# Recurrent stage of a two-block transformer: inverses of 16 x 16 diagonal blocks by substitution on VectorE, moved through DRAM

## The chip, the cores and the metric

The kernel runs on one core of a Trainium2 chip. The metric is the device time of one execution in microseconds. All times below are in microseconds unless marked ns; a time such as 1224.23 is counted from the start of the profiled span.

## The reference

The program is one forward pass of a block with attention and an expert layer, then two further layers. The change touches the mixer of the first of these, which has a recurrent part (8 heads of 64) and a "stick-breaking" attention (8 heads) side by side:

```
def step(state, inp):
    r_t, w_t, k_t, v_t, kk_t, a_t = inp
    sa = jnp.einsum('bhij,bhj->bhi', state, -kk_t)
    state = (state * w_t[:, :, None, :] + sa[..., None] * (kk_t * a_t)[:, :, None, :]
             + v_t[..., None] * k_t[:, :, None, :])
    return state, jnp.einsum('bhij,bhj->bhi', state, r_t)
...
_, y = lax.scan(step, state0, (tm(r), tm(decay), tm(k), tm(v), tm(kk), tm(a)))
```

The sequence has 256 tokens. The kernel does the scan in two chunks of 128 tokens. Within a chunk each head needs the inverse of a unit triangular 128 x 128 matrix I + N, where N holds the products of kk and of kk * a for pairs of tokens, strictly on one side of the diagonal.

## The kernel before

All of this is in `stage_hyb`. Eight heads and two chunks give 16 matrices; they are handled as four groups `(t, g)`, chunk t and head parity g, of four matrices j side by side in a [128, 4, 128] tile.

The stage first runs projections on TensorE: `w_hr` and its small companions, then `w_hq` (queries and keys of the stick attention, `lin_b`, evicted to `sqkT`) and `w_hv` (its values, `lin_a`, into `acc` banks and then `sv`). Their weights come by SP's DMA queue into three `raw` buffers; ScalarE copies each piece of 1024 columns to `hi`, VectorE subtracts to get `lo` (L303), and both must be there before TensorE uses the piece. A further load is issued once the buffer of three loads earlier has been split. While the projections run, VectorE makes the decay-weighted keys and queries `bet`, `kti`, `kap`.

After the projections two streams are written side by side, step by step: `stick()`, with for each of 8 heads the steps logits (tile `psb`), sums (`psc` from `ab`) and values (`sbo`), and `chain()`. `chain()` computes N by `scores` (four groups of four products, masked by `upS` into `NT`), makes the inverses of the diagonal blocks of 2 by a mask, and then doubles the block: for b = 2, 4, 8, 16, 32 there are a product with N (`psq`, L1407, masked into `room`), a product with the transposed inverse (`pst`, L1413, subtracted from `T`), and sixteen transposes that renew `TT` (`ptt`, L1419). A shorter last level joins blocks of 64. Then three more sets of `scores` give the matrices with which rows, states and outputs are computed (`psrh`, `psu`, `pss`, `psy`), interleaved with the output projection `pho`.

A scheduler orders the instructions of each engine over the whole stage by its own estimates; what it chose is shown below as it stands in the built programs. Within one engine, and within SP's queue, instructions run in that order, and one that waits holds all behind it. From `rows_of` on TensorE's order is written by hand.

GpSimd applies two masks to every stick head (`keep`, `nb`; the matrices `ntri`, `nones` are made there too) and computes the output gate (`gadd`, `gv`).

Of the kernel before, what the change touches and what calls it, by code (L numbers as in the profile page):

```python
# [13 lines left out]
F32 = mybir.dt.float32  # L14
# [6 lines left out]
OP = mybir.AluOpType  # L21
# [164 lines left out]
def block_kernel(ctx: ExitStack, tc: tile.TileContext, a: dict, out: bass.AP, start=0, stop=99):  # L186
    nc = tc.nc
# [17 lines left out]
    def bank(name="bank"):  # L205
        return pp.tile([128, 512], F32, name=name, tag="bank")
# [10 lines left out]
    def col(name, j=0, n=None):  # L217
        o, w = COLS[name]
        return cols[:, o + j:o + j + (n or 1)]
# [214 lines left out]
    class Prep:  # L434


        full = None
# [700 lines left out]

    def stage_hyb():
        DEC = math.exp(-0.5)  # L1140
        LEVELS = (2, 4, 8, 16, 32, 64)
        with ExitStack() as es:
            per = es.enter_context(pool("hper", 1))
            esB = ExitStack()
# [16 lines left out]

            upS = tri("upS", OP.is_gt, 1)
            upI = tri("upI", OP.is_ge, 1)

            b2n = per.tile([128, 64, 2], F32, name="b2n")
            G.memset(b2n, 0.0)
            G.affine_select(out=b2n[:, :, 1], in_=b2n[:, :, 1], pattern=[[-2, 64]], compare_op=OP.not_equal, fill=-1.0, base=0, channel_multiplier=1)
            b2n = b2n.rearrange("p a b -> p (a b)")

            lm = {}  # L1170
            for b in LEVELS[:-1]:
# [24 lines left out]
            qkT = per.tile([128, 8, 256], F32, name="sqkT")  # L1196
            sv = per.tile([128, 2, 512], F32, name="sv")
            oT = (per.tile([128, 4, 256], F32R, name="hoTh"), per.tile([128, 4, 256], F32R, name="hoTl"))
            bet = pb.tile([128, 4, 256], F32, name="bet")
            kti = pb.tile([128, 4, 256], F32, name="kti")  # L1200

# [39 lines left out]


            sig = pc.tile([128, 4, 256], F32, name="sig")
            at = bet
            for m in range(4):
                ps = bank("pslw")
                ps_2 = bank("psla")
# [48 lines left out]
            for b in range(2):  # L1296
                ps = bank("psnb")
                for m in range(2):
                    T.matmul(ps[:, m * 256:(m + 1) * 256], sel[:, 2 * b + m, :], rnT, start=True, stop=True)
                V.tensor_tensor(out=kap[:, 2 * b:2 * b + 2, 0, :], in0=kap[:, 2 * b:2 * b + 2, 0, :],  # L1300
                                in1=ps.rearrange("p (m n) -> p m n", m=2), op=OP.mult)

            for m in range(4):
                V.tensor_scalar(out=tmp[:, m, :], in0=at[:, m, :], scalar1=-1.0, scalar2=col("k_a", m), op0=OP.add, op1=OP.mult)
            V.scalar_tensor_tensor(out=kti, in0=tmp, scalar=1.0, in1=kti, op0=OP.add, op1=OP.mult)
            V.tensor_tensor(out=bet, in0=kk, in1=at, op=OP.mult)
            iE = expo(L3, DEC)
            V.tensor_tensor(out=bet, in0=bet, in1=iE, op=OP.mult)
            eX = expo(sig, -DEC)
            V.tensor_tensor(out=kk, in0=kk, in1=eX, op=OP.mult)  # L1310

            for m in range(4):
                V.scalar_tensor_tensor(out=tmp[:, m, :], in0=kap[:, m, 1, :], scalar=col("r_k", m), in1=kti[:, m, :], op0=OP.mult, op1=OP.mult)
# [19 lines left out]
            def cons_qk(m0, mc, ps):  # L1333
                V.tensor_tensor(out=qkT[:, m0:m0 + mc, :], in0=ps.rearrange("p (m n) -> p m n", n=256),
                                in1=rb().unsqueeze(1).to_broadcast([128, mc, 256]), op=OP.mult)

            lin_b("w_hq", 8, 8, 2, xT, cons_qk, bank=acc)

# [8 lines left out]
            ch2 = esD.enter_context(pool("hch2", 2))  # L1347

            table = tc.keep_in_program_order(nc.scalar.preload_act_table_set("natural_log_exp_and_others"))
            TG = [(t, g) for t in range(2) for g in range(2)]  # L1350
            po_ = lambda g: slice(g * 64, (g + 1) * 64)
            b4 = lambda m: m.unsqueeze(1).to_broadcast([128, 4, 128])
            j4 = lambda ps: ps.rearrange("p (j n) -> p j n", j=4)

            room = hT.tile([128, 2, 16, 128], F32, name="room", tag="T8")
            room = [room[:, n] for n in range(2)]
# [1 line left out]
            def mat(name, tag=None):  # L1358
                return ch.tile([128, 4, 128], F32, name=name, tag=tag or name)

            def mat2(i, t, g):

                return room[i][:, 4 * (2 * t + g):4 * (2 * t + g) + 4, :]

            def scores(l, r, t, g):

                ps = bank("psc")
                ts = slice(t * 128, (t + 1) * 128)
                for j in range(4):
                    T.matmul(ps[:, j * 128:(j + 1) * 128], l(j)[po_(g), ts], r(j)[po_(g), ts], start=True, stop=True)  # L1370
                return j4(ps)

            vb, vk = (lambda j: bet[:, j, :]), (lambda j: kti[:, j, :])
            vq, vr = (lambda j: kap[:, j, 0, :]), (lambda j: kap[:, j, 1, :])
            NT, Tm, TT, Bm, LB, LK, U = {}, {}, {}, {}, {}, {}, {}
            btk, htk = ch.tile([128, 512], F32, name="btk"), ch.tile([128, 512], F32, name="htk")

            def chain():

                for t, g in TG:  # L1380
                    ps = scores(vb, vq, t, g)
                    NT[t, g] = mat(f"NT{t}{g}")
                    V.tensor_tensor(out=NT[t, g], in0=ps, in1=b4(upS), op=OP.mult)
                    TT[t, g] = mat(f"TT{t}{g}")
                    V.tensor_tensor(out=TT[t, g], in0=NT[t, g], in1=b4(b2n), op=OP.mult)
                    V.tensor_tensor(out=TT[t, g], in0=TT[t, g], in1=b4(ident), op=OP.add)
                yield
                for t, g in TG:
                    ps = bank("ptt")
                    for j in range(4):  # L1390
                        T.transpose(ps[:, j * 128:(j + 1) * 128], TT[t, g][:, j, :], ident)
                    Tm[t, g] = mat(f"T{t}{g}")
                    A.copy(out=Tm[t, g], in_=j4(ps))
                yield
                to_tok(bet, btk, 0)
                to_tok(kti, htk, 0)
                yield
                for b in LEVELS[:-1]:
                    nb = 64 // b
                    half = lambda x, h: x.rearrange("p j (c h s) -> p j c h s", h=2, s=b)[:, :, :, h, :]  # L1400
                    Q = {}
                    for t, g in TG:
                        Q[t, g] = mat2(0, t, g)
                        G.memset(half(Q[t, g], 1), 0.0)
                        ps = bank("psq")
                        for j in range(4):
                            T.matmul(ps[:, j * 128:(j + 1) * 128], NT[t, g][:, j, :], Tm[t, g][:, j, :], start=True, stop=True)  # L1407
                        V.tensor_tensor(out=half(Q[t, g], 0), in0=half(j4(ps), 0), in1=lm[b].unsqueeze(1).to_broadcast([128, 4, nb, b]), op=OP.mult)
                    yield
                    for t, g in TG:  # L1410
                        ps = bank("pst")
                        for j in range(4):
                            T.matmul(ps[:, j * 128:(j + 1) * 128], TT[t, g][:, j, :], Q[t, g][:, j, :], start=True, stop=True)  # L1413
                        V.tensor_tensor(out=half(Tm[t, g], 0), in0=half(Tm[t, g], 0), in1=half(j4(ps), 0), op=OP.subtract)
                    yield
                    for t, g in TG:
                        ps = bank("ptt")
                        for j in range(4):
                            T.transpose(ps[:, j * 128:(j + 1) * 128], Tm[t, g][:, j, :], ident)  # L1419
                        A.copy(out=TT[t, g], in_=j4(ps))  # L1420
                    yield
                lo, hi = slice(0, 64), slice(64, 128)
                for t, g in TG:
                    Q[t, g] = mat2(0, t, g)
                    ps = bank("psq")
                    for j in range(4):
                        T.matmul(ps[hi, j * 64:(j + 1) * 64], NT[t, g][lo, j, hi], Tm[t, g][lo, j, lo], start=True, stop=True)
                    A.copy(out=Q[t, g][hi, :, 0:64], in_=ps[hi, 0:256].rearrange("p (j n) -> p j n", j=4))
                yield
                for t, g in TG:  # L1430
                    ps = bank("pst")
                    for j in range(4):
                        T.matmul(ps[lo, j * 64:(j + 1) * 64], Q[t, g][hi, j, 0:64], TT[t, g][hi, j, hi], start=True, stop=True)
                    A.activation(out=TT[t, g][lo, :, hi], in_=ps[lo, 0:256].rearrange("p (j n) -> p j n", j=4), func=AF.Copy, scale=-1.0)
                yield
                for dst, l, r, m, tag in ((Bm, vk, vq, upS, None), (LK, vk, vr, upI, "T"), (LB, vb, vr, upI, "NT")):
                    for t, g in TG:
                        ps = scores(l, r, t, g)
                        d = dst[t, g] = mat(f"B{t}{g}", f"{tag}{t}{g}") if tag else mat2(1, t, g)
                        if dst is LB:  # L1440
                            A.copy(out=d, in_=ps)
                            G.affine_select(out=d, in_=d, pattern=[[0, 4], [1, 128]], compare_op=OP.is_ge, fill=0.0, base=0, channel_multiplier=-1)
                        else:
                            V.tensor_tensor(out=d, in0=ps, in1=b4(m), op=OP.mult)
                yield
# [617 lines left out]
```

## Time and profile before

| what | value |
|---|---|
| median of 3 runs (lowest to highest) | 1897.76 (1897.35 to 1899.72) |
| profiled execution, its own time | 1900.1 |
| its span | 1897.9 |
| TensorE busy | 1841.0 (97% of the span) |
| VectorE busy | 1467.2 (77%) |
| ScalarE busy | 998.5 (53%) |
| GpSimd busy | 119.5 (6%) |
| granted TensorE clock, mean | 0.986 of full |

The profiler records one execution. Busy time is the time in which an engine had an instruction under way; TensorE's matmuls overlap, so their durations add up to more than the time that passes, and the time of a step is read from one start to the next. The granted clock is 1.0 at 2.4 GHz and 0.5 at 1.2 GHz.

### The profile page before, as it was taken

How to read it: one execution, taken by the hardware profiler on the slowest of the kernel's cores; microseconds unless marked ns; L12 is line 12 of the kernel's file. 1: busy time of each engine (PE TensorE's matmuls, PEld its weight loads, DVE VectorE, ACT ScalarE, POOL GpSimd, SP SyncE). 2: the span in 40 equal slices, each digit the busy share in tenths (PEclk: the TensorE clock that was granted, in tenths of full speed). 3: DMA queues.
4: the chain of work that ended last, by engine and by line, in shares of the span. 5: the costliest groups of instructions: out<-in, count | busy, mean ns of one | idle time of the engine just before them, and what ended most of it. 6: DMA issues, size and time to landing. Idle time of an engine off the chain costs nothing.

```text
span 1897.9 us, 28745 instructions
## 1 busy us (share of the span) xinstructions
PE 1841.0 (97%) x10944; PEld 1559.8 (82%) x10944; DVE 1467.2 (77%) x3076; ACT 998.5 (53%) x1702; POOL 119.5 (6%) x195
## 2 busy tenths in 40 slices
PE   8999979799999999999999999999999999999997
PEld 6777769798888888888888898898788889688886
DVE  7786766989999887888776588544787888687787
ACT  6566455333555555555555454442555566665555
POOL 0000003330000000000000202222000000000000
PEclk9999999999999999999999999999999999999999
DMA  7442533344555555555555543101455544155552
GB/s 272 168 156 92 177 120 112 112 140 172 178 178 178 178 178 178 178 179 190 179 195 179 190 164 127 68 7 51 150 193 185 173 169 166 71 186 180 197 178 100
DMA packets 43754, 296.13 MB, mean 156 GB/s; under 512 B 4896, under 2 KB 5040, under 8 KB 10208
## 3 DMA queue, kind: packets, MB, share of 16 engines
q1 hardware_dynamic: 41872, 289.35, 43.9%
q0 software_dynamic: 1184, 3.89, 0.7%
q8 instruction: 86, 1.41, 0.3%
q10 hardware_dynamic: 560, 1.05, 0.1%
q14 instruction: 52, 0.43, 0.1%
HBM read 293.23 MB, written 1.05 MB: 155 GB/s over the span
## 4 chain that ended last, share of the span: by engine, by line
PE 89%; DVE 6%; ACT 2%; issue 1%; DMA 1%; POOL 0%; SPq 0%; ACTq 0%; POOLq 0%; DVEq 0%
PE psf L343 9%; PE psa L343 9%; PE po L336 6%; PE po L338 6%; PE po L337 6%; PE psf L346 4%; PE psa L346 4%; PE acc L337 4%; PE acc L338 4%; PE acc L336 4%; PE psa L923 3%; PE psb L336 2%; PE psb L338 2%; PE psb L337 2%; PE go L337 2%; PE go L336 2%
## 5 line engine op out<-in xcount | busy, mean ns | idle before, releaser
L303 DVE TENSOR_TENSOR lo<-raw,hi 128x1024 fp32r<-128x1024 f32 (+3 forms) x511 | 617.0, 1209 | 181.5 <-ACT hi L301 172.8
L301 ACT ACTIVATE hi<-raw 128x1024 fp32r<-128x1024 f32 (+3 forms) x531 | 555.8, 1049 | 304.8 <-PE acc L338 94.2
L343 PE MATMUL psf<-xT,hi 128*128 128x512 f32 x704 | 250.9, 401 | 1.6 <-DVE xT L412 1.6
L343 PE MATMUL psa<-xT,hi 128*128 128x512 f32 x704 | 248.0, 396 | 0.0
L336 PE MATMUL po<-hi,gx 128*128 128x512 f32 x512 | 206.1, 403 | 0.8 <-ACT gx L1090 0.8
L337 PE MATMUL po<-lo,gx 128*128 128x512 f32 x512 | 202.0, 394 | 0.0
L338 PE MATMUL po<-hi,gx 128*128 128x512 f32 x512 | 201.6, 394 | 0.0
L346 PE MATMUL psf<-xT,lo 128*128 128x256 f32 x704 | 184.7, 283 | 0.0
L346 PE MATMUL psa<-xT,lo 128*128 128x256 f32 x704 | 183.1, 281 | 0.0
L343 PEld LDWEIGHTS psf<-xT,hi 128*128 128x128 f32 x704 | 130.5, 190 | 27.8 <-DVE xT L412 1.8
L343 PEld LDWEIGHTS psa<-xT,hi 128*128 128x128 f32 x704 | 129.3, 188 | 25.6
L346 PEld LDWEIGHTS psf<-xT,lo 128*128 128x128 f32 x704 | 134.3, 191 | 8.1
L346 PEld LDWEIGHTS psa<-xT,lo 128*128 128x128 f32 x704 | 132.8, 189 | 7.9
L338 PEld LDWEIGHTS po<-hi,gx 128*128 128x128 f32 x512 | 96.4, 188 | 22.7 <-DVE gx L1091 0.3
L336 PEld LDWEIGHTS po<-hi,gx 128*128 128x128 f32 x512 | 96.4, 188 | 20.9 <-ACT gx L1090 1.0
L337 PEld LDWEIGHTS po<-lo,gx 128*128 128x128 f32 x512 | 96.6, 189 | 20.4
L337 PE MATMUL acc<-lo,xT 128*128 128x512 f32 (+3 forms) x288 | 110.9, 385 | 0.2
L336 PE MATMUL acc<-hi,xT 128*128 128x512 f32 (+3 forms) x288 | 110.8, 387 | 0.0
L338 PE MATMUL acc<-hi,xT 128*128 128x512 f32 (+3 forms) x288 | 109.6, 381 | 0.0
L913 ACT COPY gl<-psa 128x256 f32<-128x256 f32 x88 | 32.8, 372 | 128.4 <-PE psa L343 128.4
L336 PE MATMUL psb<-xT,hi 128*128 128x256 f32 (+1 forms) x312 | 91.4, 294 | 2.1 <-DVE hrb L549 1.1
L338 PE MATMUL psb<-xT,lo 128*128 128x256 f32 (+1 forms) x312 | 90.8, 291 | 0.0
(646 smaller groups left out, 3682.2 us busy)
## 6 DMA issues: line engine op xcount, KB each, us to landing
raw<-in_u_dram SPq DMA_DIRECT2D x64, 1024.0 KB, 4.9
raw<-in_v_dram SPq DMA_DIRECT2D x64, 1024.0 KB, 4.9
raw<-in_w_f_dram SPq DMA_DIRECT2D x44, 1024.0 KB, 4.8
raw<-in_w_fo_dram SPq DMA_DIRECT2D x22, 1024.0 KB, 4.8
raw<-in_w_in_dram SPq DMA_DIRECT2D x17, 1024.0 KB, 5.0
raw<-in_w_pg_dram SPq DMA_DIRECT2D x8, 1024.0 KB, 4.8
raw<-in_w_hr_dram SPq DMA_DIRECT2D x6, 1024.0 KB, 5.2
raw<-in_w_out_dram SPq DMA_DIRECT2D x4, 1024.0 KB, 4.9
```

Source lines behind the costliest of these rows:

```text
L301: A.activation(out=hi[:, :w], in_=r, func=AF.Copy)
L303: ins = eng.tensor_tensor(out=lo[:, :w], in0=r, in1=hi[:, :w].bitcast(F32), op=OP.subtract)
L336: T.matmul(ps, l[0], r[0], start=first, stop=False, skip_group_check=not check)
L337: T.matmul(ps, l[0], r[1], start=False, stop=False, skip_group_check=not check)
L338: T.matmul(ps, l[1], r[0], start=False, stop=last, skip_group_check=not check)
L343: hi = lambda: T.matmul(ps, w[0], x.both[:, :, k, :], start=first, stop=last, skip_group_check=not check)
L346: T.matmul(ps[:, 0:256], w[1], x.hi[:, k, :], start=False, stop=False, skip_group_check=not check)
L913: A.copy(out=g[:, m], in_=ps[:, 256:512])
L923: T.matmul(ps[:, m * 256:(m + 1) * 256], w[0], x32[:, k, :], start=k == 0, stop=k == 7)
```

## The change

The levels 2, 4 and 8 leave `chain()`. In their place the inverses of the 16 x 16 diagonal blocks are computed by forward substitution on VectorE, one block on each partition (16 matrices x 8 blocks = 128). The blocks get there through DRAM: eight DMAs write the diagonal blocks of N, 16 partitions x 16 matrices x 16 floats each, one load brings them back as [128, 16, 16], 30 operations of VectorE invert them, one DMA writes the result and eight DMAs scatter it into `Tms`, whose other parts are zero. For this N is computed earlier, during the projections, and `at` gets a buffer of its own. `chain()` begins by transposing `Tms` and goes on with b = 16.

```diff
-        LEVELS = (2, 4, 8, 16, 32, 64)
+        LEVELS = (16, 32, 64)
...
+            NTs, Tms = (pb.tile([128, 16, 128], F32, name=n) for n in ("NTs", "Tms"))
+            NB, X = (pc.tile([128, 16, 16], F32, name=n) for n in ("NBk", "XBk"))
+            XU = pc.tile([128, 64], F32, name="XU")
+            G.memset(Tms, 0.0)
+            G.memset(X, 0.0)
+            G.memset(X.rearrange("p i c -> p (i c)")[:, 0:256:17], 1.0)
...
-            at = bet
+            at = pc.tile([128, 4, 256], F32, name="atT")
...
+            for t, g in TG:
+                V.tensor_tensor(out=NT[t, g], in0=scores(vb, vq, t, g), in1=b4(upS), op=OP.mult)
...
+            def diagonal(full, blk, back):
+                z = dr.tile([8, 16, 16, 16], F32, name=f"blk{back:d}")
+                if back:
+                    nc.sync.dma_start(z.rearrange("b q i c -> (b q) i c"), blk)
+                for b in range(8):
+                    bs = slice(16 * b, 16 * b + 16)
+                    f, d = full[bs, :, bs], z[b].rearrange("q i c -> i q c")
+                    nc.sync.dma_start(*((f, d) if back else (d, f)))
+                if not back:
+                    nc.sync.dma_start(blk, z.rearrange("b q i c -> (b q) i c"))
+
+            def inverses():
+                for k in range(15):
+                    n = 15 - k
+                    u = XU[:, 0:n * (k + 1)].rearrange("p (i c) -> p i c", c=k + 1)
+                    V.tensor_tensor(out=u, in0=NB[:, k, k + 1:16].unsqueeze(2).to_broadcast([128, n, k + 1]),
+                                    in1=X[:, k, 0:k + 1].unsqueeze(1).to_broadcast([128, n, k + 1]), op=OP.mult)
+                    V.tensor_tensor(out=X[:, k + 1:16, 0:k + 1], in0=X[:, k + 1:16, 0:k + 1], in1=u, op=OP.subtract)
+                diagonal(Tms, X, True)
+
+            diagonal(NTs, NB, False)
...
+                if m0 == 2:
+                    inverses()
...
-                for t, g in TG:
-                    ps = scores(vb, vq, t, g)
-                    NT[t, g] = mat(f"NT{t}{g}")
-                    V.tensor_tensor(out=NT[t, g], in0=ps, in1=b4(upS), op=OP.mult)
-                    TT[t, g] = mat(f"TT{t}{g}")
-                    V.tensor_tensor(out=TT[t, g], in0=NT[t, g], in1=b4(b2n), op=OP.mult)
-                    V.tensor_tensor(out=TT[t, g], in0=TT[t, g], in1=b4(ident), op=OP.add)
-                yield
                 for t, g in TG:
                     ps = bank("ptt")
                     for j in range(4):
-                        T.transpose(ps[:, j * 128:(j + 1) * 128], TT[t, g][:, j, :], ident)
-                    Tm[t, g] = mat(f"T{t}{g}")
-                    A.copy(out=Tm[t, g], in_=j4(ps))
+                        T.transpose(ps[:, j * 128:(j + 1) * 128], Tm[t, g][:, j, :], ident)
+                    TT[t, g] = mat(f"TT{t}{g}")
+                    A.copy(out=TT[t, g], in_=j4(ps))
```

SP's DMA queue, from the loads of the values' weights (`w_hv`) to the first loads of the next layer (`w_f`); a row is line, operation, destination and source, and shape, with - for the kernel before and + for the change:

```order
 L284 DMA raw<-in_w_hv_dram 128x2048 x2
-L284 DMA raw<-in_w_ho_dram 128x2048 x4
-L284 DMA raw<-in_w_f_dram 128x2048 x3
+L284 DMA raw<-in_w_ho_dram 128x2048
+L1339 DMA blk_11657<-NTs 16x16x16 x8
+L284 DMA raw<-in_w_ho_dram 128x2048
+L1341 DMA NBk<-blk_11657 128x256
+L284 DMA raw<-in_w_ho_dram 128x2048 x2
+L284 DMA raw<-in_w_f_dram 128x2048
+L1335 DMA blk_11852<-XBk 128x256
+L1339 DMA Tms<-blk_11852 16x16x16 x8
```

The eighteen new DMAs stand among the weight loads: the loads of `w_ho` and `w_f` now follow waits for N and for the inverses.

TensorE before, from the end of the values' projection (`acc`) to the start of the first level; L1469 and L1470 are a head's logits, L1484 to L1486 its sums:

```order
L338 MATMUL acc<-hi,xT 128x512
L1469 MATMUL psb<-sqkT 128x256
L1470 MATMUL psb<-sqkT 128x128
L1370 MATMUL psc<-kap,bet 128x128 x16
L1469 MATMUL psb<-sqkT 128x256
L1470 MATMUL psb<-sqkT 128x128
L1391 MATMUL ptt<-ident,TT_12037 128x128 x4
L1484 MATMUL psc_12110<-ab,ntri 128x256
```

TensorE in the change, from sums of the second head to the first product of level 16; L1496 and L1497 are logits, L1511 to L1513 sums, L1523 and L1524 values:

```order
L1513 MATMUL psc_12221<-ab,nones 128x128
L1523 MATMUL sbo<-z,sv 64x256
L1524 MATMUL sbo<-z,sv 64x128
L1496 MATMUL psb<-sqkT 128x256
L1497 MATMUL psb<-sqkT 128x128
L1523 MATMUL sbo<-z,sv 64x256
L1524 MATMUL sbo<-z,sv 64x128
L1418 MATMUL ptt<-ident,Tms 128x128 x16
L1373 MATMUL pstk<-ident,bet 128x128 x4
L1373 MATMUL pstk<-ident,kti 128x128 x4
L1434 MATMUL psq<-Tms,NTs 128x128 x16
```

The products for N have left this place, and four logits, two sums and two values of the stick attention now stand ahead of the transposes of `Tms`, which wait for the last of the eight DMAs.

VectorE in the change, at the end of the projections (L303 is a weight split, `XU` and `XBk` the substitution, the last row the first step of the stick attention):

```order
L1381 TENSOR_TENSOR sqkT<-psb,hrb 128x512
L303 TENSOR_TENSOR lo<-raw,hi 128x1024
L1348 TENSOR_TENSOR XU<-NBk,XBk 128x15
L1350 TENSOR_TENSOR XBk<-XBk,XU 128x15
L303 TENSOR_TENSOR lo<-raw,hi 128x1024
...
L1348 TENSOR_TENSOR XU<-NBk,XBk 128x15
L1350 TENSOR_TENSOR XBk<-XBk,XU 128x15
L1501 SCALAR_TENSOR_TENSOR ab<-z 128x384 x2
```

Before, four weight splits stood there by themselves; now the thirty operations stand among them (two more splits are in the part left out), and the stick attention's rows stand behind the last.

## Rows read from the trace of the kernel before

**Rows 1.** The page's chain that ended last: shares of the span by engine.
```profile
PE 89%; DVE 6%; ACT 2%; issue 1%; DMA 1%; POOL 0%; SPq 0%; ACTq 0%; POOLq 0%; DVEq 0%
```

**Rows 2.** By stretch: us, then busy PE, PEld, DVE, ACT, POOL; clock, DMA share, GB/s.
```profile
1199.00:1213.30 14.30, 12.11 (x75) 10.55 (x75) 11.65 (x19) 8.94 (x17) 4.08 (x7) 0.77 0.21 74
...
1224.20:1271.30 47.10, 47.10 (x378) 43.69 (x377) 20.70 (x46) 17.29 (x35) 11.54 (x20) 1.00 0.01 1
```

**Rows 3.** Timeline of TensorE, level 4: start, us, line, operation, count, idle before.
```profile
1224.23 0.70 PE L1469 MATMUL psb<-sqkT 64*128 64x256 f32 x2
...
1225.07 3.84 PE L1407 MATMUL psq<-T,NT 128*128 128x128 f32 x32
1228.75 0.60 PE L1484 MATMUL psc<-ab,ntri 128*128 128x256 f32 x2
...
1229.63 3.74 PE L1413 MATMUL pst<-room,TT 128*128 128x128 f32 x32
1233.29 0.65 PE L1496 MATMUL sbo<-z,sv 128*64 128x256 f32 x2
...
1234.09 1.97 PE L1419 MATMUL ptt<-ident,T 128*128 128x128 f32 x16
1235.98 0.70 PE L1469 MATMUL psb<-sqkT 64*128 64x256 f32 x2
```

**Rows 4.** Timeline of TensorE, from the projections' end to the first level.
```profile
1199.73 2.72 PE L1370 MATMUL psc<-kap,bet 64*128 64x128 f32 x32
...
1205.91 0.70 PE L1484 MATMUL psc<-ab,ntri 128*128 128x256 f32 x2 [1.83 <-POOL ab L1478]
...
1208.82 3.04 PE L1391 MATMUL ptt<-ident,TT 128*128 128x128 f32 x12
1211.65 1.06 PE L1326 MATMUL pstk<-ident,bet 128*128 128x128 f32 x4
```

**Rows 5.** Timeline of VectorE, two places; then two of its groups by shape.
```profile
1171.94 0.17 DVE L1318 COPY rkr<-psrk 128x16 f32<-128x16 f32 x1 [1.00 <-PE psrk L1317]
...
1175.15 2.06 DVE L1310 TENSOR_TENSOR kap<-kap,expo 128x1024 f32<-128x1024 f32 x1
...
1311.31 0.17 DVE L244 TENSOR_TENSOR rs_t<-gnr 128x8 f32<-128x8 f32 x1
1311.51 0.17 DVE L245 TENSOR_TENSOR rs_t<-rs_t,rs_v 128x8 f32<-128x8 f32 x1
...
L303 DVE TENSOR_TENSOR lo<-raw,hi 128x1024 fp32r<-128x1024 f32 x52 | 63.5, 1224 | 24.0 <-ACT hi L301 23.9
...
L1383 DVE TENSOR_TENSOR NT<-psc,upS 128x512 f32<-128x512 f32 x4 | 2.7, 684 | 2.1 <-PE psc L1370 2.1
```

**Rows 6.** Timeline of GpSimd beside VectorE's products.
```profile
1173.09 3.03 POOL L1527 TENSOR_TENSOR gadd<-vtk,rkr 128x512 f32<-128x512 f32 x2 [14.46 <-ACT vtk L1327]
```

**Rows 7.** DMA: SP's issues at the start; queues of 0 to 12; landings by issue.
```profile
1.73 0.46 SPq L284 DMA_DIRECT2D raw<-in_w_in_dram  x1
...
2.23 1.17 SPq L284 DMA_DIRECT2D raw<-in_w_in_dram  x2
...
q10 hardware_dynamic: 272, 0.52, 11.6%
q0 software_dynamic: 64, 0.03, 0.8%
...
w2a<-in_w2a_dram POOLq DMA_DIRECT2D x1, 256.0 KB, 3.0
...
DMA to landing us min/median/max: 2.0/2.3/2.5
```

**Rows 8.** Timeline of ScalarE, its last weight copy before the projections end.
```profile
1196.36 1.06 ACT L301 ACTIVATE hi<-raw 128x1024 fp32r<-128x1024 f32 x1 [1.66 <-PE acc L338]
```

**Rows 9.** The same view of 3 us ahead of the first level.
```profile
1207.00:1210.00 3.00, 3.00 (x12) 2.37 (x12) 3.00 (x5) 0.52 (x2) 0.26 (x1) 0.50 0.00 0
```

**Rows 10.** Timeline of ScalarE, the exponential of the head of rows 3.
```profile
1230.48 0.52 ACT L1488 ACTIVATE z<-z 128x384 f32<-128x384 f32 x1 [3.05 <-DVE z L1487]
```

More of the change, by code (lines that the diff above doesn't have):

```diff
@@ L1140, in stage_hyb @@
         DEC = math.exp(-0.5)
-        LEVELS = (2, 4, 8, 16, 32, 64)
+        LEVELS = (16, 32, 64)
+        TG = [(t, g) for t in range(2) for g in range(2)]
+        po_ = lambda g: slice(g * 64, (g + 1) * 64)
+        b4 = lambda m: m.unsqueeze(1).to_broadcast([128, 4, 128])
+        j4 = lambda ps: ps.rearrange("p (j n) -> p j n", j=4)
         with ExitStack() as es:
@@ L1163, in stage_hyb @@
             upI = tri("upI", OP.is_ge, 1)
[L1165 to L1168, printed above, removed]
             lm = {}
@@ L1198, in stage_hyb @@
             oT = (per.tile([128, 4, 256], F32R, name="hoTh"), per.tile([128, 4, 256], F32R, name="hoTl"))
+            NTs, Tms = (pb.tile([128, 16, 128], F32, name=n) for n in ("NTs", "Tms"))
+            NT, Tm = ({(t, g): z[:, 4 * (2 * t + g):4 * (2 * t + g) + 4, :] for t, g in TG} for z in (NTs, Tms))
+            NB, X = (pc.tile([128, 16, 16], F32, name=n) for n in ("NBk", "XBk"))
[3 more added lines that the diff above has]
+            G.memset(X.rearrange("p i c -> p (i c)")[:, 0:256:17], 1.0)
             bet = pb.tile([128, 4, 256], F32, name="bet")
@@ L1301, in stage_hyb @@
                                 in1=ps.rearrange("p (m n) -> p m n", m=2), op=OP.mult)
-            for m in range(4):
-                V.tensor_scalar(out=tmp[:, m, :], in0=at[:, m, :], scalar1=-1.0, scalar2=col("k_a", m), op0=OP.add, op1=OP.mult)
-            V.scalar_tensor_tensor(out=kti, in0=tmp, scalar=1.0, in1=kti, op0=OP.add, op1=OP.mult)
             V.tensor_tensor(out=bet, in0=kk, in1=at, op=OP.mult)
@@ L1310, in stage_hyb, with scores @@
             V.tensor_tensor(out=kk, in0=kk, in1=eX, op=OP.mult)
+            def scores(l, r, t, g):
+                ps = bank("psc")
+                ts = slice(t * 128, (t + 1) * 128)
+                for j in range(4):
+                    T.matmul(ps[:, j * 128:(j + 1) * 128], l(j)[po_(g), ts], r(j)[po_(g), ts], start=True, stop=True)
+                return j4(ps)
+            vb, vk = (lambda j: bet[:, j, :]), (lambda j: kti[:, j, :])
+            vq, vr = (lambda j: kap[:, j, 0, :]), (lambda j: kap[:, j, 1, :])
+            for t, g in TG:
+                V.tensor_tensor(out=NT[t, g], in0=scores(vb, vq, t, g), in1=b4(upS), op=OP.mult)
+            dr = esC.enter_context(tc.tile_pool(name="hdr", bufs=1, space=bass.MemoryType.DRAM))
+            def diagonal(full, blk, back):
[17 more added lines that the diff above has]
+            diagonal(NTs, NB, False)
+            for m in range(4):
+                V.tensor_scalar(out=tmp[:, m, :], in0=at[:, m, :], scalar1=-1.0, scalar2=col("k_a", m), op0=OP.add, op1=OP.mult)
+            V.scalar_tensor_tensor(out=kti, in0=tmp, scalar=1.0, in1=kti, op0=OP.add, op1=OP.mult)
             for m in range(4):
@@ L1349, in stage_hyb @@
             table = tc.keep_in_program_order(nc.scalar.preload_act_table_set("natural_log_exp_and_others"))
[L1350 to L1353, printed above, removed]
             room = hT.tile([128, 2, 16, 128], F32, name="room", tag="T8")
@@ L1363, in mat2 @@
                 return room[i][:, 4 * (2 * t + g):4 * (2 * t + g) + 4, :]
[L1365 to L1375, printed above, removed]
+            TT, Bm, LB, LK, U = {}, {}, {}, {}, {}
             btk, htk = ch.tile([128, 512], F32, name="btk"), ch.tile([128, 512], F32, name="htk")
@@ L1435, in chain @@
                 yield
-                for dst, l, r, m, tag in ((Bm, vk, vq, upS, None), (LK, vk, vr, upI, "T"), (LB, vb, vr, upI, "NT")):
+                for dst, l, r, m, place in ((Bm, vk, vq, upS, None), (LK, vk, vr, upI, Tm), (LB, vb, vr, upI, NT)):
                     for t, g in TG:
                         ps = scores(l, r, t, g)
-                        d = dst[t, g] = mat(f"B{t}{g}", f"{tag}{t}{g}") if tag else mat2(1, t, g)
+                        d = dst[t, g] = place[t, g] if place else mat2(1, t, g)
                         if dst is LB:
```

## Prediction

> **What bounds the kernel now.** I read four things: the chain that ended last, busy time by stretch, TensorE's rows in the recurrent chain, and the engines and queues that the new work would stand on. The chain of the whole program is 89% TensorE [rows 1], so time is saved only where TensorE has less to do or waits less. The change touches one stage, from about 1148 us on. Before 1199 us TensorE does projections there, from 1199 us the chain with the stick attention between its steps. By stretch [rows 2], TensorE is busy 12.1 of 14.3 us between 1199.0 and 1213.3 (2.2 us idle) and never idle from 1224.2 to 1271.3, with ScalarE and VectorE under half busy. So in the levels TensorE is the bound, and the waits lie ahead of the first level.
>
> One level as TensorE sees it [rows 3]: product with N from 1225.07, then a head's sums from 1228.75, product with the transposed inverse from 1229.63, a head's values from 1233.29, sixteen transposes from 1234.09, the next head's logits from 1235.98. From logits (1224.23) to logits (1235.98) is 11.75 us. Of these the stick attention takes 0.84 (1224.23 to 1225.07), 0.88 (1228.75 to 1229.63) and 0.80 (1233.29 to 1234.09), which makes 2.52. The level itself is 11.75 - 2.52 = 9.23 us.
>
> **What it removes.** Levels 2, 4 and 8 go: 3 x 9.23 = 27.7 us of the engine that sets the end. The stick steps between them do not go. They stay on TensorE, 2.52 us a head.
>
> **What it moves at no price, and under which cover.** The sixteen products for N (2.72 us, rows 4) move from the chain's head into the projection's stream. TensorE is the bound in both places, so the sum is 0. The projection then ends near 1201.7, not 1199.0. This needs the operands to be there when TensorE arrives, near 1175.5 (46 matmuls of 0.12 after 1170.0). On VectorE the product into kap ended at 1177.2 [rows 5]. Ahead of it now stands one more 0.68 us row, but gone are the idle 1.0 us for psrk and GpSimd's two gadd, which took 3.03 us beside a product of 2.06 us [rows 5, 6], where other rows of 1024 elements take 1.2 [rows 5]. So 1175.3: just in time. If the product and its neighbour stay that slow, TensorE waits some 1.5 us. The removed multiply, add and masks were on VectorE and GpSimd, which are not the bound.
>
> **What it adds: a loop N, DRAM, VectorE, DRAM, TensorE.** I follow it to P, the time at which the transposes of Tms can start.
> N: after 1175.3 come a weight row (1.2), a product of 1024 (1.2) and four masks (0.68 each): 1180.5.
> First scattered set, S: eight DMAs of 256 pieces of 64 B. No row before has such pieces. Issues stand 0.5 us apart, and a write to DRAM lands 2.3 us after its issue [rows 7]. So S is at least 7 x 0.5 + 2.1 = 5.6 us. Each of the 16 DMA engines has 8 x 16 = 128 pieces. Queue 10 took 11.6% of 16 x 12 us for 272 packets, 0.082 us each, for pieces of 2 KB; queue 0, with the smallest packets, took 0.024 us [rows 7]. At 0.082, S is 128 x 0.082 + 2.1 = 12.6. These pieces are small, like queue 0's, but go to DRAM one by one, which no row does; I take the middle, S = 9. N is in DRAM at 1189.5.
> NB: a load of 256 KB landed in 3.0 us [rows 7], so 1192.5. VectorE gets there at about 1192 by itself, behind a weight split. It waits little.
> Inverses: thirty dependent operations. Dependent rows of 8 elements follow each other every 0.20 us, and a row costs about 1.03 ns more for each element (684 ns for 512, 167 for 8) [rows 5]. 30 x 0.20 + 1360 x 0.00103 = 7.4 us. Three weight splits of 1.2 us stand between them, and the last waits for ScalarE's copy, which waits for TensorE: 1196.4 before [rows 8], so 2.7 later now, ending at 1200.1. After it 1.2 + 13 operations of 0.23 remain: 1204.4.
> Back: the write stands behind a weight load on SP (5 us, issued about 1202) and lands near 1208; then S again. P = 1208 + 9 = 1217.
>
> Who waits meanwhile: the splits of the next weights stand behind NB on VectorE, but are for products after 1290. On SP the loads of these weights stand behind the same waits, with the same slack. The first stick heads are not so free. Their first VectorE row stands behind the last inverse, and the tile ntri reuses memory that the write back reads, so GpSimd's masks start at 1208. Two heads then give their values at about 1216.6, by steps of 0.5 to 1.0 us. So P is 1217 if S is 9, and 1216.6 if S is 5.6. Above S = 9 it is 1180.5 + S + 3 + 7.4 + 3.6 + 2.7 + S = 1197.2 + 2S, so 1222.4 for 12.6.
>
> TensorE between 1201.7 and P has 4 logits, 2 sums and 2 values: 3.4 + 1.8 + 1.6 = 6.8 of 15.3 us. Idle 8.5, against 2.2 before: +6.3 us (+11.7 at S = 12.6).
>
> **The clock.** After the idle 1.83 us at 1204 [rows 4] the granted clock fell to 0.50, that is 1.2 GHz, from 1207 on [rows 9]; twelve transposes took 2.83 us from start to start where sixteen take 1.9 [rows 3, 4]. By such pairs the slow level cost 3.4 us before the first level (twelve transposes 1.4, the eight of pstk 0.85, logits and sums together 1.15). Now the sixteen transposes (1.9) and eight more (0.85) would run at it: 2.75. Difference -0.6. The Trainium skill ("TensorE: Matmul & The Clock Gate", Part 1) says that the throttled state is the default and activity releases it. Both kernels pay it once by these rows, so the sum stands; by the rule alone, 15 us of sparse work would run slow throughout, which is idle time anyway.
>
> **The tail.** Four heads (4 to 7) now lie beside and behind level 64 and the last scores. One head from logits to values takes 1224.23 to 1233.29 when covered. In the new order 3.8 us of psrh, psu and output products stand between their steps; following them I find about 1 us uncovered: +1.0.
>
> **Sum.** -27.7 + 6.3 - 0.6 + 1.0 = -21.0 us. The profiled execution took 1900.1 us (span 1897.9, 2.2 around it), so it would be 1879.1. The median of the runs is 1897.8, 2.3 below; the forecast is in its terms: 1897.8 - 21 = 1876.8.
>
> **Rivals.**
> A, all of it: S at its lower end, the idle time and the slow clock no worse than before, tail covered: -27.7, so 1870.1. For it: projections could hide the loop. Against: GpSimd's masks wait for the write back whatever S is. 10%.
> B, the heads lose their cover: the levels hid the heads' latency. If each of heads 4 to 7 takes 7.6 us (4.5 from logits to sums, 1224.23 to 1228.75; 2.25 to the end of its exponential, 1231.00 [rows 10]; 0.8 for values), of which TensorE works 2.5, then 4 x 5.1 = 20.4 idle, less 7.1 of psrh, psu and pho between: 13.3 in place of 1.0. 1876.8 + 12.3 = 1889.1. For it: one GpSimd runs 2 us of masks a head, and the gate products stand ahead of heads 5 to 7 there. Against: the new order interleaves three heads. 13%.
> C, the scattered pieces decide, the other side: from S = (1217 + 21 - 1197.2)/2 = 20.4 us on, the kernel is slower. If a 64 B piece costs twice the 0.082 us packet, S = 128 x 0.164 + 2.1 = 23.1, P = 1243.4, 26.4 later: 1903.2, slower by 5.4. For it: these pieces are the one thing that no row shows. Against: the small packets of queue 0 at 0.024. 8%. The Trainium skill ("DMA: Bandwidth & Descriptors", Specifications) says that below 512 B a DMA does read-modify-write; with two passes a piece it gives this case.
> In 4% something else, such as TensorE short of split weights in the projection.
>
> **Numbers.** Forecast 65%, its own range 1872 to 1883 (S from 5.6 to 12.6, tail up to 3 us less or more). A 10%, B 13%, C 8%. The range for 8 in 10 takes in A and B: 1870 to 1890. 0.2%, 3.8 us, is about what a measurement of this kernel can tell from no change: faster by more (forecast, A, B) 0.88, within it 0.04, slower 0.08.
>
> **What would show it.** The stretch from the projection's end to the first transposes of Tms: about 15 us, more than half idle, ended by a DMA. VectorE's inverses: about 11 us with three splits. Each scattered set 5.6 to 12.6 us from first issue to last landing. Two levels of 9.2 us. The last scores end about 30 us earlier, the state products 21 earlier, and the rest shifts unchanged. It is wrong if a set takes over 20 us, if TensorE stalls within the projection, or if idle time in the tail exceeds 5 us.

## The result, and the profile after

Medians: 1875.82 us after, 1898.02 before, ratio 0.9882 [0.9868, 0.9897]. A later repeat of the unaltered kernel gave 1879.30 against 1898.07, 0.9891 [0.9869, 0.9912]. So 22.2 and 18.8 us were saved; 21.0 was forecast. The profiled span is 1875.3 us.

TensorE still carries the chain, as in [rows 1]:

```profile
PE 88%; DVE 7%; ACT 2%; issue 1%; DMA 1%; POOL 0%; SPq 0%; ACTq 0%; POOLq 0%; DVEq 0%
```

The loop, by SP's timeline (start, us, line, operation, count), then the landings in the same stretch (KB each, median us from issue to landing), then the DMA queues from 1179.8 to 1185.3:

```profile
1179.89 5.39 SPq L1339 DMA_DIRECT2D blk<-NTs  x8
1186.60 0.34 SPq L1341 DMA_DIRECT2D NBk<-blk  x1
1204.74 0.33 SPq L1335 DMA_DIRECT2D blk<-XBk  x1
...
blk<-NTs SPq DMA_DIRECT2D x8, 16.0 KB, 1.7
NBk<-blk SPq DMA_DIRECT2D x1, 128.0 KB, 4.4
blk<-XBk SPq DMA_DIRECT2D x1, 128.0 KB, 2.3
Tms<-blk SPq DMA_DIRECT2D x8, 16.0 KB, 1.9
...
q1 hardware_dynamic: 1635, 0.10, 16.3%
```

The eight issues span 5.4 us, and each lands 1.7 us (the median) after its start; NB's load, which waits for the whole set, is issued 6.7 us after the first. The pieces cost little: 16.3% of 16 engines for 5.5 us over 1635 packets is 8.8 ns of one DMA engine each. So the issues on SP set the length of a set, not the pieces.

VectorE's first and last substitution rows, and GpSimd's first rows behind the write back (in brackets the idle time before and its releaser):

```profile
1193.05 0.17 DVE L1348 TENSOR_TENSOR XU<-NBk,XBk 128x15 f32<-128x15 f32 x1
...
1204.49 0.18 DVE L1350 TENSOR_TENSOR XBk<-XBk,XU 128x15 f32<-128x15 f32 x1
...
1207.18 0.20 POOL L1477 MEMSET ntri<- 128x128 f32 x1 [4.29 <-DMA blk<-XBk]
1209.71 0.99 POOL L1505 TENSOR_TENSOR ab<-ab,keep 128x384 f32<-128x384 f32 x1
```

TensorE, where [rows 3, 4] showed it before:

```profile
1201.69 0.71 PE L1496 MATMUL psb<-sqkT 64*128 64x256 f32 x4
...
1210.75 1.22 PE L1511 MATMUL psc<-ab,ntri 128*128 128x256 f32 x2 [8.13 <-POOL ab L1505]
...
1219.30 1.97 PE L1418 MATMUL ptt<-ident,Tms 128*128 128x128 f32 x16
...
1221.98 3.74 PE L1434 MATMUL psq<-Tms,NTs 128*128 128x128 f32 x32
...
1230.87 3.74 PE L1434 MATMUL psq<-Tms,NTs 128*128 128x128 f32 x32
...
1240.74 0.68 PE L1454 MATMUL psq<-Tms,NTs 64*64 64x64 f32 x8
...
1254.36 0.65 PE L1523 MATMUL sbo<-z,sv 128*64 128x256 f32 x2
...
1270.31 0.70 PE L1511 MATMUL psc<-ab,ntri 128*128 128x256 f32 x2 [1.45 <-POOL ab L1505]
...
1274.76 0.33 PE L1595 MATMUL pss<-U,btk 128*64 128x64 f32 x2
```

In the kernel before, the first row behind the last scores and the first state products (`pss`) were these:

```profile
1285.52 0.70 PE L1484 MATMUL psc<-ab,ntri 128*128 128x256 f32 x2
...
1295.27 0.33 PE L1568 MATMUL pss<-U,btk 128*64 128x64 f32 x2
```

The stretches behind TensorE's wait in the changed kernel (columns as in [rows 2]):

```profile
1207.00:1210.00 3.00, 0.00 (x0) 0.00 (x0) 0.91 (x2) 0.26 (x1) 2.82 (x10) 0.53 0.24 22
1210.00:1213.00 3.00, 2.25 (x7) 1.85 (x8) 0.07 (x1) 0.00 (x0) 3.00 (x4) 0.50 0.24 22
1213.00:1216.00 3.00, 3.00 (x10) 2.41 (x10) 1.50 (x2) 1.01 (x2) 2.56 (x3) 0.50 0.03 5
1216.00:1219.00 3.00, 3.00 (x13) 1.86 (x13) 1.11 (x2) 1.95 (x4) 1.25 (x2) 0.76 0.00 0
1219.00:1222.00 3.00, 3.00 (x28) 2.83 (x27) 1.32 (x2) 2.49 (x7) 0.71 (x1) 1.00 0.00 0
```

Ahead of the transposes of `Tms`, TensorE waits once, 8.13 us, for a head's mask on GpSimd. The heads' products then run at a granted clock of 0.50 (1.2 GHz), and the transposes start 7 us after the blocks landed (the last issue at 1210.4, and 1.9 to its landing, make 1212.3), at full clock. The levels' products start at 1221.98, 1230.87 and 1240.74. The scores end 31.2 us earlier than before (1254.36 against 1285.52), the state products start 20.5 earlier (1274.76 against 1295.27).

Behind the stage the first profile gained another 4.3 us up to 1358 (of which 2.1 were left at the end: the spans differ by 22.6). Here is the same work, about 20 us earlier in the changed kernel: the kernel before, the change, and the change in its repeat:

```profile
1320.00:1330.00 10.00, 7.47 (x29) 5.54 (x28) 6.73 (x20) 2.44 (x4) 0.00 (x0) 0.83 0.17 73
1341.00:1351.00 10.00, 8.08 (x31) 6.83 (x32) 6.97 (x24) 4.22 (x12) 0.00 (x0) 0.66 0.39 148
...
1300.00:1310.00 10.00, 7.47 (x35) 5.60 (x35) 8.29 (x22) 3.16 (x6) 0.84 (x5) 1.00 0.12 51
1320.00:1330.00 10.00, 8.45 (x49) 7.19 (x48) 6.36 (x23) 3.99 (x12) 0.00 (x0) 1.00 0.28 105
...
1300.00:1310.00 10.00, 7.82 (x25) 5.53 (x24) 7.15 (x21) 2.46 (x5) 0.17 (x3) 0.66 0.08 34
1320.00:1330.00 10.00, 7.53 (x38) 6.24 (x36) 7.74 (x25) 4.99 (x13) 0.00 (x0) 0.83 0.46 183
```

In the repeat the stage is the same (state products 73.08 us behind the projections' end, against 73.07), but the slow stretches are back, and the span is 4.2 longer. TensorE's longest wait for ScalarE there, for `hobTh`, is 1.20 us in all three. So these 4 us come and go from one execution to the next and are not the change's.

### The profile page after: what moved, and what is told of

The parts are those of the page before. It is cut to its first block, busy times and chain, and to the rows that moved or that the text cites. A ratio compares the mean times of both kernels' runs of the same rounds, so it can differ in the third digit from the quotient of the medians.

```text
span 1875.3 us, 28222 instructions
## 1 busy us (share of the span) xinstructions
PE 1810.1 (97%) x10704; PEld 1529.5 (82%) x10704; DVE 1457.4 (78%) x3074; ACT 991.2 (53%) x1690; POOL 106.8 (6%) x175
## 4 chain that ended last, share of the span: by engine, by line
PE 88%; DVE 7%; ACT 2%; issue 1%; DMA 1%; POOL 0%; SPq 0%; ACTq 0%; POOLq 0%; DVEq 0%
PE psf L343 9%; PE psa L343 9%; PE po L336 7%; PE po L338 6%; PE po L337 6%; PE psf L346 4%; PE psa L346 4%; PE acc L337 4%; PE acc L338 4%; PE acc L336 4%; PE psa L923 3%; PE psb L336 2%; PE psb L338 2%; PE psb L337 2%; PE go L336 2%; PE go L337 2%
## 5 line engine op out<-in xcount | busy, mean ns | idle before, releaser
L303 DVE TENSOR_TENSOR lo<-raw,hi 128x1024 fp32r<-128x1024 f32 (+3 forms) x511 | 617.3, 1210 | 177.4 <-ACT hi L301 168.7
```

What stands on the lines that cost most here:

```text
L303: ins = eng.tensor_tensor(out=lo[:, :w], in0=r, in1=hi[:, :w].bitcast(F32), op=OP.subtract)
```

## The experiments

The order on TensorE comes from the scheduler, so every variant first needs a base that holds it. All offsets (+) count from the projections' end, which is the start of TensorE's next product behind them. The kernel before, measured beside each: 1897.39 for c0, e1, e3 and e5, 1894.88 for e6 to e9, 1898.07 for e10. From one profile to the next the projections' end comes at 1197.8 to 1201.7, and from the state products to the end it takes 599.0 (c0) to 605.2 us (e6). So the offsets within the stage tell more than medians a few us apart.

**c0_held.** The start of TensorE's order (L logits, S sums, V values of a head, C a chain step) written out (code cut):

```
FIRST = "L0 L1 S0 L2 S1 V0 L3 V1 C C C C C C C S2 C".split()
with tc.manual_schedule(engines={mybir.EngineType.PE}):
    for x in FIRST: next(st if x[0] in "LSV" else ch_)
```

> The changed kernel with TensorE's order around the first transposes of Tms written by hand as the scheduler chose it (a head's logits and one head's values move by a few products). It is the base for the experiments that follow, and shows what repeats from run to run. Every theory: 1875.8 within 0.3%, first transposes of Tms at 1219.3, one idle stretch of TensorE of 8.1 us before the first sums, granted clock 0.50 after it. Whether the two stretches at 0.50 that the kernel before had behind the stage (near 1326 and 1344) come back or not is open: if they are chance, they may appear here; if the change removed them, they don't.

Measured 1882.81, 0.9937 [0.9912, 0.9962] (the medians alone give 0.9923; one of ten executions took 1902.52): not the same kernel. Transposes +17.52 (after +17.61), scores' end +53.68 (+52.67), but state products +82.20 (+73.07). GpSimd's timeline, then TensorE's, then its clock:

```profile
1248.09 1.01 POOL L1506 TENSOR_TENSOR z<-z,nb 128x384 f32<-128x384 f32 x1
1249.03 0.58 POOL L229 DMA_DIRECT2D room<-in_ln_b_dram  x1
1252.67 2.49 POOL L1556 TENSOR_TENSOR gadd<-gadd,room 128x512 f32<-128x512 f32 x2 [3.07 <-DMA room<-in_ln_b_dram]
...
1263.34 0.99 POOL L1505 TENSOR_TENSOR ab<-ab,keep 128x384 f32<-128x384 f32 x1
...
1264.39 1.22 PE L1511 MATMUL psc<-ab,ntri 128*128 128x256 f32 x2 [2.64 <-POOL ab L1505]
...
1264.00:1274.00 10.00, 9.61 (x31) 7.18 (x31) 2.05 (x5) 2.33 (x5) 3.23 (x4) 0.50 0.00 0
```

The load of ln_b is issued behind a head's masks here; in the changed kernel it was issued ahead of them (at 1247.25, the masks at 1248.44). The gate products start 2.8 us later, and the next head's mask stands behind them. TensorE waits 2.64 us, where its longest wait in the tail was 1.45, and the clock falls: the state products come 9.1 us later. How long it stays down varies: e1 and e3 have this order on GpSimd too and wait 2.50 and 2.61 in the same place, but there the clock is 0.83 over the 10 us behind the wait, and the state products come at +77.10 and +77.60. So the order costs 4 to 9 us.

**e1_masks_apart.** The tile XBk in another pool, so that GpSimd's masks no longer wait for the write back:

```
-NB, X = (pc.tile([128, 16, 16], F32, name=n) for n in ("NBk", "XBk"))
+NB, X = (p.tile([128, 16, 16], F32, name=n) for p, n in ((pc, "NBk"), (pb, "XBk")))
```

> XBk in a pool of its own life, so that GpSimd's ntri no longer takes over memory that the write back still reads; order of TensorE as in the base. Theory now (the chain goes from the write back to GpSimd's masks to the sums; the scattered DMAs end earlier): masks made by 1205.5, then gadd, the first head's mask at 1207.5 and no longer at 1209.7, first transposes of Tms at 1217.1, 2.2 us earlier, time 2.2 lower. Rival, the theory of the prediction that a DMA of Tms ends the wait: no change, because the write back and the eight DMAs stay where they are.

Measured 1883.04, 0.9920 [0.9893, 0.9947]. The masks were made by +4.2, yet the first sums came at +8.81 (c0 +9.06) and the transposes at +17.51: 2.2 us were expected, 0.25 came at the sums and none at the transposes. VectorE, then GpSimd:

```profile
1205.48 2.71 DVE L1504 SCALAR_TENSOR_TENSOR ab<-z,ab 128x384 f32<-128x384 f32 x2
...
1204.46 3.32 POOL L1554 TENSOR_TENSOR gadd<-vtk,rkr 128x512 f32<-128x512 f32 x2
```

After, these took 1.03 and 2.03 us, apart from each other. The Trainium skill ("GPSIMD Engine Reference", Specifications) says that GpSimd shares its SBUF interfaces with VectorE, with contention for VectorE instructions with two SBUF inputs; these rows agree. The wait removed came back as slower work side by side.

**e3_sixteen.** Sixteen DMAs of half a block back, not eight:

```
-for b in range(8):
+for b, r in [(b, r) for b in range(8) for r in range(1 + back)]:
...
```

> The inverses go into Tms by sixteen DMAs of half a block in place of eight; order of TensorE as in the base. At 0.5 us an issue the last lands at 1216.5 and not at 1212.5. Theory now: still ahead of TensorE, which works on the heads until 1219.3, so no change. Rival, the prediction's sum in which the set on the way back stands in the chain: first transposes and time 4.0 us later.

Measured 1881.83, 0.9926 [0.9909, 0.9942]. The issues into `Tms` span 5.79 us where they spanned 3.76, 2.0 more, and the transposes came 0.4 later (+17.93). The blocks have slack: S on the way back doesn't set P, the time at which the transposes start.

**e5_warm, e7_warm32.** 64 or 32 products of ident on TensorE ahead of the first sums:

```
+for _ in range(64):   # e7: 32
+    T.matmul(wps[:, 0:128], ident, ident, start=True, stop=True)
```

> 64 products of ident with itself, whose result nothing reads, are put on TensorE between the first two heads' logits and the first sums, where it was idle (64 x 0.11 = 7.2 us of 8.1); the rest as in the base. Theory: the clock stays at 1.00, the two sums, two logits and values behind the wait run at full rate; by the rates of the levels the first transposes of Tms come at 1215.9, 3.4 us earlier, and the time is 3.4 lower. Rival (the heads' own chain through GpSimd, VectorE and ScalarE sets their pace, not TensorE's rate): under 1 us. A second rival (the products delay the sums): later by up to 1 us.

> As the base, with 32 products of ident with itself, whose result nothing reads, between the first logits and the first sums (64 of them took 14.6 us and delayed the sums by 6.2, but held the clock at 1.00: from the first sums to the transposes 5.6 us in place of 8.5). 32 take 7.3 of the 8.1 us idle. Theory: first sums at the same place as in the base, transposes of Tms 2.9 us earlier. Rival (the wait itself, not the clock, sets that stretch): no change.

Measured 1884.98, 0.9943 [0.9925, 0.9961], and 1882.87, 0.9939 [0.9919, 0.9959]. The 64 took 14.56 us (0.227 each), the 32 took 7.41; the clock stayed at 1.00 up to the transposes in both. From first sums to transposes: 8.46 in c0, 5.60, 6.60. So the slow clock costs the heads up to 2.9 us. With 64 products the sums were 6.2 later, which took back more. With 32 products 1.10 came back as a wait for ScalarE's z, and the first sums were 1.3 later, as was GpSimd's mask: the transposes came at +16.99, 0.5 earlier and not 2.9, and the time was not lower. Of the stretch up to the transposes the clock is the smaller part and the wait for the mask the larger.

**e6_gates_behind.** The gate products on GpSimd behind the last head's mask:

```
+with tc.issue_after(masks[-1].ins):
     for t in range(2):
         gates(t)
```

> As the base, but GpSimd does its gate products (gadd, gv, some 10 us) behind the last head's masks and not ahead of the masks of heads 5 to 7. In the base GpSimd worked on them from 1252.7 to 1263.3, TensorE waited 2.6 us for a head's mask behind them, then ran at granted clock 0.50 for 10 us, and the state products came 8.0 us later than in the changed kernel. Theory (the order on GpSimd decides the tail; the heads lost their cover by it): the wait goes, the clock stays at 1.00, from the last scores to the state products 19 to 20.5 us in place of 28.4, time 8 to 9 lower than the base's. Rival (each head's own chain over four engines sets the pace, whatever stands on GpSimd): 2 to 3 us lower at most.

Measured 1874.78, 0.9888 [0.9870, 0.9905]; state products +73.02, 9.2 earlier than in c0, 4.1 and 4.6 earlier than in e1 and e3. By the medians 20.1 us under the kernel before, where c0 was 14.6 under it: a gain of 5.5, and 8 to 9 were expected. TensorE in the tail:

```profile
1268.51 0.70 PE L1513 MATMUL psc<-ab,ntri 128*128 128x256 f32 x2 [1.51 <-POOL ab L1507]
```

One wait of 1.51, clock 1.00 from the scores to the state products. So GpSimd's order decides the tail.

**e8_level8.** On e6, level 8 put back:

```
-LEVELS = (16, 32, 64)
+LEVELS = (8, 16, 32, 64)
```

> As the run with the gate products behind the masks, and one level of the chain put back (blocks of 8, after the inverses of 16 are in place; its subtraction hits parts already done, so the output is not the reference's). Theory: a level is worth what the trace says wherever it stands, 8.9 to 9.2 us more than that run. Rival (the level covers heads' waits, so that taking it out gains less): under 7 us more.

Measured 1887.12, 0.9950 [0.9931, 0.9969]. The scores end 9.02 later than in e6 (+62.66, +53.64). A level is worth what the rows said. The state products come 10.6 later (+83.62), for behind the same wait of 1.51 us as in e6 the clock fell here (0.83 in 1276 to 1286). The medians differ by 12.3; the rest is not settled.

**e9_best.** On e6: the mask of the last scores on VectorE, more chain work ahead of the transposes, half of the scattered DMAs on ScalarE's queue, the heads spread.

```
+(nc.scalar if b % 2 else nc.sync).dma_start(*((f, d) if back else (d, f)))
...
+V.tensor_tensor(out=d, in0=ps, in1=b4(m), op=OP.mult)
```

> A version put together from what the runs showed: gate products behind the masks; the mask of the last scores on VectorE in place of GpSimd; the scattered DMAs from two queues; the transposes of bet and kti and the first of the three late sets of scores, which need no inverse, written ahead of the transposes of Tms, that is into TensorE's idle time; the heads' steps spread by hand over the levels. Theory: Tms lands about 9 us after the projections' end and not 11, its transposes follow at once (17.5 before); TensorE has some 4 us idle left of 8.1; state products 65 to 68 us after the projections' end, against 73.1 in the changed kernel; time 5 to 8 lower than that kernel. If the heads' own chain sets the pace instead, the state products stay near 73.

Measured 1871.95, 0.9880 [0.9858, 0.9903]; transposes +11.58, state products +69.68, 1.7 behind the range expected. SP:

```profile
1200.49 0.33 SPq L284 DMA_DIRECT2D raw<-in_w_f_dram  x1
1201.28 0.33 SPq L1335 DMA_DIRECT2D blk<-XBk  x1
1207.54 1.80 SPq L1339 DMA_DIRECT2D Tms<-blk  x4
```

The write back, issued 0.8 us behind a load of 1 MB, landed after 6.2 us, not 2.3, and TensorE waited 1.9 for Tms.

**e10_loads_behind.** e9 on one queue, the weight loads ordered behind the blocks:

```
+if name == "w_ho" and moved:
+    tc.add_manual_dep(ld.ins, moved[-1].ins.name, NoSync, ...)
```

> From the version put together before: there the write back of the inverses, issued 0.8 us after a weight load on the same queue, landed 6.2 us after its issue, where it took 2.2 in the base, issued 3.0 us after the load; and ScalarE, which issued half of the DMAs, stood 3.9 us in front of them. Now all DMAs of the blocks are on SP again, and the four loads of the output projection's weights (first used some 50 us later) stand on SP behind the last DMA into Tms, so that their splits leave the thirty operations of VectorE alone too. Theory: NB lands 2.3 us after its issue and not 4.4; the inverses take 7.4 us and not 11.6 and end before the projections do; the write back takes 2.3; Tms is there 3 us after the projections' end, its transposes run at 4 to 5 us behind the transposes and scores that were put ahead (17.5 in the base, 11.6 in the version before), TensorE has no idle stretch and the clock stays at 1.00; state products 58 to 62 us after the projections' end (73.1 in the changed kernel); time about 12 lower than the changed kernel's. Rival (the heads' chain over GpSimd, VectorE and ScalarE sets the pace as soon as TensorE has no other wait): state products at 66 or later.

Measured 1867.50, 0.9845 [0.9828, 0.9862], 11.8 under the unaltered change on the same chip, of which the stage shows 8.5 (state products +64.56 against +73.08). SP and TensorE:

```profile
1194.84 0.34 SPq L1337 DMA_DIRECT2D blk<-XBk  x1
1196.56 4.68 SPq L1341 DMA_DIRECT2D Tms<-blk  x8
1201.35 12.71 SPq L284 DMA_DIRECT2D raw<-in_w_ho_dram  x4
...
1203.47 1.99 PE L1427 MATMUL ptt<-ident,Tms 128*128 128x128 f32 x16
1207.43 5.47 PE L1440 MATMUL psq<-Tms,NTs 128*128 128x128 f32 x32 [1.97 <-ACT TT L1429]
```

Inverses took 7.2 us with no split between them, the write back landed in 1.7, the transposes came at +5.71. The state products came 2.6 behind the range expected, for a wait of 1.97 for ScalarE's copies and a half-clock stretch behind it.

## Why the prediction was right

The mechanism held in the main. Three levels of TensorE's work went, and a wait for a loop through VectorE and GpSimd took back part of it.

- Levels: 9.23 each by the rows; e8 measured 9.02. -27.7 stands as about -27.
- N moved ahead: its products started at 1175.36 (1175.5 forecast) without a wait of TensorE, and the projections' end came at 1201.69 (1201.7).
- The loop: masks 1179.9 (1180.5), inverses 11.6 us to 1204.7 (11, 1204.4), write back at 1207.1 (1208). NB took 4.4, not 3.0, which VectorE's own arrival at 1193 hid.
- **S was mis-sized**: 6.7 and 5.3 us for 9. The middle was a choice between bounds 24 and 82 ns a piece; 8.8 was under both. (Its sums also take 2.1 us for a landing, where their row says 2.3.) Rival C is refuted here. The Trainium skill ("DMA: Bandwidth & Descriptors", Specifications) says that below 512 B a DMA does read-modify-write; no run shows whether these pieces did, only that they were cheap.
- **"Ended by a DMA" was wrong**, the step that failed: GpSimd's masks ended the wait. With S small, the prediction's own branch gave 1216.6 by the heads; P came at 1219.30. The slow clock can account for most of these 2.7 us (1.9 by e7, 2.9 by e5): I put it on the transposes (2.75 us), but the heads' rows ahead of them ran in it and the transposes at 1.00. The first product of level 16 was forecast at 1217 + 5.5 = 1222.5 (twenty-four transposes, 2.75 at full clock and as much again at the slow one) and came at 1221.98: two errors that cancel, which is luck. Idle time was 8.13 for 8.5.
- Tail: 1.45 us of wait for 1.0. Rival B did not come, but its mechanism is real: c0 shows GpSimd's slack there to be under 2.8 us, with 4 to 9 us behind it (e1, e3, c0).
- Rest "shifts unchanged": the stage gave 20.5 of 21.0. With the measured terms the sum is -27.1 + 5.9 (idle 8.13 for 2.2) - 0.5 (clock 2.9 for 3.4) + 1.45 (tail) = -20.2. What the two medians differ by, and the 4 us behind the stage, are not settled by a term of the sum.

What stays open: why waits of one length, in the tail and behind the stage, drop the clock in one profile and not in another, and for longer in one than in another.

## What to carry to other kernels

When work leaves the bounding engine for a round trip, follow what queues behind that trip on every engine: here GpSimd's masks, not the data, ended the wait. Before you trust a tail, look at what stands ahead of its smallest step on the slowest engine; where the gate products stood in GpSimd's order was worth 4 to 9 us. A small transfer on the path should not be issued behind large loads that have slack.

## What the hardware showed unexpectedly

- Pieces of 64 B from SBUF to DRAM cost 8.8 ns of one DMA engine each; a set of 2048 took as long as its eight issues and one landing (6.7 us, and 5.3 on the way back).
- A write of 128 KB landed in 1.7 us with no load ahead (e10), 2.3 us when it was issued 3.0 us behind a 1 MB load (the change), 6.2 us when 0.8 us behind one (e9).
- In the tail a wait of 2.64 us was followed by 17 us at 0.50 (c0), while waits of 2.50 and 2.61 were followed by 10 us at a mean of 0.83 (e1, e3). Waits of 1.45 and 1.51 left the clock at 1.00 (the change, e6), but in e8 it fell behind a wait of 1.51 too.
- GpSimd and VectorE side by side slow each other (e1): 1.36 us where a row takes 0.52 on VectorE alone, 1.66 where it takes 1.02 on GpSimd alone.
